# A two-layer trunk on one core: smaller sets of weight tiles, sums on VectorE, 1/rms by tokens, three plain pairs

## The chip, the cores and the metric

The kernel runs on one core of a Trainium2 chip. The metric is the device time of one execution in microseconds (us); lower is better. Engines are named as the profile names them: PE is TensorE (matmuls), PEld its weight loads, DVE VectorE, ACT ScalarE, POOL GpSimd, SP SyncE, which issues most DMAs. Times in rows of the timeline are counted from the start of the profiled span.

## What is computed

A stack of two layers over 1056 tokens (1024 of a prompt and 32 of a running stream), width 1024. Each layer adds a token mixer and then an MLP to the stream h, and the end is one more rmsnorm:

```python
def rmsnorm(x, g):
    y = x * lax.rsqrt(jnp.mean(x * x, axis=-1, keepdims=True) + EPS)
    return y * g

def short_conv_mixer(h, buf, w_in, conv_w, w_out):      # layer 1's mixer
    bg, cg, u = jnp.split(h @ w_in, 3, axis=-1)
    zc = jnp.concatenate([buf, cg * u], axis=1)
    conv = sum(zc[:, j:j + T] * conv_w[j] for j in range(CONV_W))
    return (bg * conv) @ w_out, zc[:, -(CONV_W - 1):]

for i in range(DEPTH):                                   # layer 0: HGRN2 recurrence, layer 1: the convolution
    a = rmsnorm(h, norm_mix[i])
    h = h + mixer_i(a)
    m = rmsnorm(h, norm_mlp[i])
    h = h + jnp.square(jax.nn.relu(m @ w_up[i])) @ w_down[i]    # 1024 -> 4096 -> 1024
return rmsnorm(h, norm_final), new states
```

All is float32 in and out.

## The kernel before

**Number format.** TensorE multiplies in a shortened float32 (`float32r`). Every operand is therefore split into a high part (a cast on ScalarE) and a low part (operand minus high part, on VectorE), and each product is three matmuls: low weights by high activations, high by low, high by high. For weights, `wsplit` does it: a DMA from SP into a tile `raw`, the cast to `whi` (L93), the subtraction into `wlo` (L94). These tiles come from the pool `ws`, which has five `whi`, five `wlo` and four `raw` of 1024 columns; a new one waits until the oldest is no longer read. For activations `split` does it: `xh[k]` on ScalarE (L182), `xl[k]` on VectorE (L183). h is kept transposed in eight tiles `hT[m]`, 128 channels by 1056 tokens.

**The MLP** (L763 to L914) goes through the hidden width in chunks of 256 channels. A group is: two up stages for a chunk (L107 to L109, 72 matmuls each), the two down stages of the chunk before, and the sums of the new one. A down stage is a 2x2 block product done with 7 instead of 8 block multiplications (L803 to L823): seven steps, each for p = 0 and 1, each of six matmuls into a PSUM tile that lives over several steps; after a step its result is added to hT, by VectorE straight from PSUM (L823), or, for steps 0 and 6, by a ScalarE copy out of PSUM (L710) and a GpSimd add (L711). The sums of weight blocks are GpSimd adds (L722) between two splits (L719 and L720, L723 and L724); those of activations are VectorE's (L749), with splits at L745 and L746. PSUM holds four tiles of two banks, all shared. Weights are asked for two stages ahead (`ready` in `mlp`). In layer 0 the last chunk's down product is done plainly: two stages make the eight rows m of hT, drained by VectorE (L840, L841), row m needing the tiles of row m - 2.

**The hand-over.** As soon as a row of hT is final, `fin0(m)` runs for it: `nrm2.add(m)` squares it on ScalarE (L649) and adds the square to a sum on GpSimd (L650), `split_h` makes xh and xl (L182, L183), and a GpSimd DMA parks the row. After every second row `tsums` makes the activation sums that the convolution's products need: scaling on ScalarE (L941), four adds on GpSimd (L943), three splits (L934 with L935, L931 with L932).

**The convolution's products** (L1125 to L1162) are twelve pairs. A plain pair is 192 matmuls (`pair_plain`), one with sums 168 (`pair_sums`); the weights of pair n + 1 are fetched and prepared (`cplain`, `csums`) while pair n multiplies. In pair 0, before its last block row of the first half, `nrm2.scale` makes 1/rms of every token as a full 128 x 1056 tile: three fp32 matmuls with a matrix of ones (L659), VectorE's scaling out of PSUM (L660) and ten more VectorE operations of 1056 columns (L134 to L139). The kernel's start does the same in another way already: `tok_rsqrt` sums over channels with the tokens on the partitions (L153, results of nine columns) and `tok_spread` spreads them again (L171 makes nine diagonal tiles, L172 multiplies them by ones).

**What sets the order.** The program is traced through a tile framework. A list scheduler orders each engine's queue from data dependences, the tracing order and estimated times; every engine then works its queue strictly in that order, with semaphores between engines. So where an instruction stands in its engine's queue is a result of the schedule, and moves when tiles or other instructions change.

## Time and profile before

| | |
|---|---|
| time, median of three runs | 2424.72 us (2424.23 to 2427.03) |
| the profiled execution | 2425.81 us, span 2424.1 us, mean granted TensorE clock 0.991 |
| busy: PE, DVE, ACT, POOL | 2364.3, 1773.4, 835.0, 805.1 us |
| layer 0's mixer, output product and first up stages | 0 to 647.6 us |
| layer 0's MLP from its first down stage | 647.6 to 1292.1 us |
| its plain stage | 1292.1 to 1324.8 us |
| the convolution's twelve pairs | 1324.8 to 1592.3 us |
| layer 1's output product and first up stages | 1592.3 to 1732.7 us |
| layer 1's MLP to its last 7-product down stage | 1732.7 to 2334.1 us |
| its last two chunks and the final norm | 2334.1 to 2424.1 us |

How to read the rows: a row of the view of waits names the engine and what it made, then what it waited for, then us in total, times and the longest. A row of the timeline is the start, the duration, the engine, the source line, the operation, `out<-in`, partitions x elements, and `xN` where N neighbours are merged; in brackets stands the idle time before it and what ended that. A row that counts forms gives the shortest, median and longest duration in ns. Matmul rows overlap, so a pace is read from starts.

### The profile page before, as it was taken

Reading aid. Unit: us, or ns where it says so; the run is one execution under the profiler, and the core shown is the slowest. Engines: PE = TensorE matmul, PEld = TensorE weight load, DVE = VectorE, ACT = ScalarE, POOL = GpSimd, SP = SyncE. Lnnn points to the kernel's source line nnn. Section 1 sums busy time; section 2 is a strip of 40 time slices with the busy share of each in tenths; the row PEclk is TensorE's granted clock in tenths of the full one; section 3 lists DMA queues with packets and bytes.
Section 4 is the critical chain, followed back from the end, with each engine's and each line's share of the span. In section 5 each row is a group of like instructions: output and inputs, shape, how many; then the busy total and the mean of one; then the engine's idle time right before and its main releaser. Section 6 shows DMA issues by size and latency. Waiting matters only on the chain.

```text
span 2424.1 us, 39880 instructions
## 1 busy us (share of the span) xinstructions
PE 2364.3 (98%) x16628; PEld 2339.6 (97%) x16628; DVE 1773.4 (73%) x2522; ACT 835.0 (34%) x1395; POOL 805.1 (33%) x837
## 2 busy tenths in 40 slices
PE   8999999999999999999998899999999999999998
PEld 8999999989999999999998899999999999999997
DVE  8876767644887877877878877644877877878855
ACT  5222222223333333333335433333433333333334
POOL 3110101022243544534537300012344534535523
PEclk9999999999999999999999999999999999999999
DMA  4101011131111111111112122231111111111102
GB/s 170 39 29 49 30 48 30 48 109 44 36 44 53 50 47 49 48 44 53 44 44 98 36 71 89 67 146 44 39 49 47 51 44 53 45 44 53 45 27 72
DMA packets 39221, 135.02 MB, mean 56 GB/s; under 512 B 4720, under 2 KB 7936, under 8 KB 39040
## 3 DMA queue, kind: packets, MB, share of 16 engines
q1 hardware_dynamic: 33632, 113.58, 14.3%
q0 software_dynamic: 5408, 18.89, 2.0%
q8 instruction: 130, 2.13, 0.4%
q14 instruction: 51, 0.42, 0.1%
HBM read 120.57 MB, written 11.88 MB: 55 GB/s over the span
## 4 chain that ended last, share of the span: by engine, by line
PE 89%; DVE 6%; ACT 2%; POOL 1%; issue 0%; DMA 0%; DVEq 0%; SPq 0%; ACTq 0%
PE pb L814 19%; PE pb L107 13%; PE pb L108 13%; PE pb L109 13%; PE pb L1033 10%; PE pj L107 4%; PE pj L108 4%; PE pj L109 4%; DVE wlo L720 2%; DVE hT L823 1%; PE v L498 1%; PE v L497 1%; DVE B L746 1%; PE v L499 1%; ACT whi L719 1%; ACT st L710 1%
## 5 line engine op out<-in xcount | busy, mean ns | idle before, releaser
L107 PE MATMUL pb<-xh,wlo 128*128 128x384 f32 (+1 forms) x1968 | 642.0, 326 | 6.1 <-DVE hT L841 3.7
L109 PE MATMUL pb<-xh,whi 128*128 128x384 f32 (+1 forms) x1968 | 637.6, 324 | 0.0
L108 PE MATMUL pb<-xl,whi 128*128 128x384 f32 (+1 forms) x1968 | 637.5, 324 | 0.0
L711 POOL TENSOR_TENSOR hT<-hT,st 128x528 f32<-128x528 f32 x232 | 375.8, 1642 | 670.4 <-ACT st L710 670.4
L823 DVE TENSOR_TENSOR hT<-hT,pb 128x528 f32<-128x528 f32 x580 | 383.9, 696 | 8.5 <-PE pb L814 0.4
L107 PEld LDWEIGHTS pb<-xh,wlo 128*128 128x128 f32 x1968 | 371.2, 189 | 8.6 <-DVE hT L841 4.0
L109 PEld LDWEIGHTS pb<-xh,whi 128*128 128x128 f32 x1968 | 371.3, 189 | 0.3
L108 PEld LDWEIGHTS pb<-xl,whi 128*128 128x128 f32 x1968 | 371.4, 189 | 0.1
L722 POOL TENSOR_TENSOR raw<-raw 128x256 f32<-128x256 f32 x232 | 227.4, 980 | 68.6 <-DVE wlo L720 57.1
L814 PE MATMUL pb<-B,whi 128*128 128x264 f32 x1392 | 226.0, 284 | 0.0
L93 ACT CAST whi<-raw 128x1024 fp32r<-128x1024 f32 (+1 forms) x119 | 123.7, 1043 | 273.3 <-PE pb L814 143.7
L789 DVE SCALAR_TENSOR_TENSOR u<-pb,nr 128x768 f32<-128x768 f32 x120 | 82.2, 703 | 166.5 <-PE pb L109 166.5
L814 PEld LDWEIGHTS pb<-B,whi 128*128 128x128 f32 x1392 | 192.6, 188 | 0.0
L107 PE MATMUL pj<-xh,wlo 128*128 128x384 f32 (+1 forms) x536 | 177.9, 332 | 7.3 <-ACT xh L182 7.3
L108 PE MATMUL pj<-xl,whi 128*128 128x384 f32 (+1 forms) x536 | 173.4, 324 | 0.0
L109 PE MATMUL pj<-xh,whi 128*128 128x384 f32 (+1 forms) x536 | 173.1, 323 | 0.0
L94 DVE TENSOR_TENSOR wlo<-raw,whi 128x1024 fp32r<-128x1024 f32 (+1 forms) x119 | 146.6, 1237 | 31.2 <-ACT whi L93 30.8
L814 PE MATMUL pb<-B,wlo 128*128 128x264 f32 x696 | 144.2, 288 | 21.3 <-DVE hT L823 21.3
L790 ACT ACTIVATE u<-u 128x768 f32<-128x768 f32 (+1 forms) x128 | 82.3, 643 | 212.8 <-DVE u L789 207.6
L814 PE MATMUL pb<-T,whi 128*128 128x264 f32 x928 | 150.8, 284 | 0.0
L814 PE MATMUL pb<-Q,whi 128*128 128x264 f32 x928 | 150.5, 284 | 0.0
L710 ACT COPY st<-pb 128x528 f32<-128x528 f32 x232 | 133.0, 600 | 46.0 <-PE pb L814 34.3
(284 smaller groups left out, 4637.1 us busy)
## 6 DMA issues: line engine op xcount, KB each, us to landing
raw<-in_wg_up_dram SPq DMA_DIRECT2D x64, 512.0 KB, 3.5
raw<-in_wg_down_dram SPq DMA_DIRECT2D x64, 512.0 KB, 3.5
raw<-in_wg_in_hgrn_dram SPq DMA_DIRECT2D x31, 512.0 KB, 4.3
raw<-in_wg_in_conv_dram SPq DMA_DIRECT2D x24, 512.0 KB, 3.5
xk<-in_x_t_dram SPq DMA_DIRECT2D x8, 528.0 KB, 8.7
hT<-in_x_t_dram POOLq DMA_DIRECT2D x8, 528.0 KB, 6.4
park<-hT POOLq DMA_DIRECT2D x8, 528.0 KB, 3.0
hT<-park POOLq DMA_DIRECT2D x8, 528.0 KB, 7.1
```

What stands on the lines that cost most here:

```text
L93: nc.scalar.copy(hi, raw)
L94: nc.vector.tensor_tensor(lo, raw, hi.bitcast(F32), op=ALU.subtract)
L107: nc.tensor.matmul(ps, wlo, ah, start=start, stop=False)
L108: nc.tensor.matmul(ps, whi, al, start=False, stop=False)
L109: nc.tensor.matmul(ps, whi, ah, start=False, stop=stop)
L710: nc.scalar.copy(q2(st), v)
L711: nc.gpsimd.tensor_tensor(d, d, st, op=op)
L722: nc.gpsimd.tensor_tensor(raw[:, d], raw[:, d], raw[:, o], op=ALU.add)
L790: nc.scalar.activation(u[:, sl], u[:, sl], AF.Square)
L814: nc.tensor.matmul(t[:, q, :QT], wf, xf[:, q * QT : (q + 1) * QT], start=start and n == 0, stop=n == 2, skip_group_check=True)
L823: nc.vector.tensor_tensor(q2(d), q2(d), v, op=op)
L1033: nc.tensor.matmul(t[:, q, :QT], w, v[:, q * QT : (q + 1) * QT], start=start and n == 0, stop=stop and n == 2, skip_group_check=True)
```

## The change

- The pool of weight tiles shrinks: four `whi` and `wlo`, three `raw`. What only the convolution needs has tiles of its own: the sums of its weights (`wsum`), and the hi and lo part of a pair's seventh factor (`whi22`, `wlo22`, two each).
- The four adds of `tsums` go from GpSimd to VectorE. `tsums` is no longer called in `fin0` but behind pairs 0 and 1, and is held back so that it is scheduled behind the instruction noted in `behind[0]`, the low part of the last row's split.
- In pair 0 `nrm2.scale` is replaced by `tok_rsqrt` (in the second half of the pair, at its third block row of the first token half) and `tok_spread` (the same of the second token half), with copies out of PSUM and the square on ScalarE.
- Pair 2 becomes plain as well (`PLAIN` 3 for 2), and `reader` gets the branch for it. `t4` follows pair 2.

```diff
...
     cp = ctx.enter_context(tc.tile_pool(name="cp", bufs=1))
     xs = ctx.enter_context(tc.tile_pool(name="xs", bufs=1))
-    ws = ctx.enter_context(tc.tile_pool(name="ws", bufs=5))
+    ws = ctx.enter_context(tc.tile_pool(name="ws", bufs=4))
     fp = ctx.enter_context(tc.tile_pool(name="fp", bufs=18))
     pj_cm = tc.tile_pool(name="pj", bufs=3, space=PSUM)
     pj = pj_cm.__enter__()
...
     def wtiles():
-        return (ws.tile([P, 4, 256], F32, tag="raw", name="raw", bufs=4),
+        return (ws.tile([P, 4, 256], F32, tag="raw", name="raw", bufs=3),
                 ws.tile([P, 4, 256], F32R, tag="whi", name="whi"),
                 ws.tile([P, 4, 256], F32R, tag="wlo", name="wlo"))
...
         rsqrt(v, y, t)
         return y
-    def tok_spread(y, n):
+    def tok_spread(y, n, new=lambda: ft("dg")):
         out = []
         for g0 in range(0, n, 512):
             ps = newps()
             for b in range(g0 // P, min(-(-n // P), g0 // P + 4)):
                 w = min(P, n - b * P)
-                dg = ft("dg")
+                dg = new()
                 nc.vector.tensor_scalar(dg[:w, :w], ident[:w, :w], y[:w, b : b + 1], None, op0=ALU.mult)
                 nc.tensor.matmul(ps[:, b * P - g0 : b * P - g0 + w], ones[:w, :], dg[:w, :w], start=True, stop=True)
             out.append((g0, min(512, n - g0), ps))
...
     parky = [dp.tile([P, NTOK], F32, name=f"parky{m}") for m in range(4)]
     half = lambda t, h: t[:, h * HALF : (h + 1) * HALF]
     TS = [{} for _ in range(4)]
+    behind = [None]
     def tpart(h, l, src, neg=False):
         if neg:
...
         for j in range(2):
             nc.scalar.activation(u[j], u[j], AF.Copy, scale=vec[:, V_NMIX + 8 + 2 * p + j : V_NMIX + 9 + 2 * p + j])
         (b11, b12), (b21, b22) = [[half(t, h) for h in range(2)] for t in u]
-        add = lambda d, a, b, op: nc.gpsimd.tensor_tensor(d, a, b, op=op)
+        add = lambda d, a, b, op: nc.vector.tensor_tensor(d, a, b, op=op)
         add(b22, b12, b22, ALU.subtract)
         add(b12, b11, b12, ALU.subtract)
         add(b11, b22, b11, ALU.subtract)
...
     def fin0(m):
         nrm2.add(m)
         split_h(m, V_NMIX + 8)
+        behind[0] = nc.cur_bb.bb.instructions[-1]
         nc.gpsimd.dma_start(out=park[m], in_=hT[m])
-        if m % 2:
-            tsums(m // 2)
     mlp(0, nrm, fin0, False)
...
         es = cv.tile([P, KT, 4], F32, name="es")
         nc.gpsimd.tensor_copy(es[:, :, 0:2], vec[:, V_SC : V_SC + 16].rearrange("p (j m) -> p m j", m=KT))
         flat = lambda t: t.rearrange("p a b -> p (a b)")
-        rawt = lambda: ws.tile([P, 4, 256], F32, tag="raw", name="raw", bufs=4)
+        rawt = lambda: ws.tile([P, 4, 256], F32, tag="raw", name="raw", bufs=3)
         hilo = lambda: [flat(ws.tile([P, 4, 256], F32R, tag=t, name=t)) for t in ("whi", "wlo")]
+        hilo22 = lambda: [cv.tile([P, 512], F32R, tag=t + "22", name=t, bufs=2) for t in ("whi", "wlo")]
         q4 = lambda t, i: t[:, i * 512 : (i + 1) * 512]
         def cfetch(n):
...
         def csums(n):
             r0, r1 = cfetch(n)
-            s = flat(rawt())
+            s = cv.tile([P, 1024], F32, name="wsum")
             a11, a12, a22, a21 = q4(r0, 0), q4(r0, 1), q4(r1, 0), q4(r1, 1)
             s1, s4 = q4(s, 0), q4(s, 1)
             add = lambda d, a, b: nc.vector.tensor_tensor(d, a, b, op=ALU.add)
...
             def put(f, src):
                 n = len(w)
                 if n % 2 == 0:
-                    t[:] = hilo()
+                    t[:] = hilo() if n < 6 else hilo22()
                 w[f] = [q4(x, n % 2) for x in t]
                 tpart(*w[f], src)
...
                 ps = [pt() for h in range(2)]
                 order = [(k, h) for k in range(KT) for h in range(2)] if mid and i == 0 else [(k, h) for h in range(2) for k in range(KT)]
                 for n, (k, h) in enumerate(order):
-                    if mid and i == 0 and n == 2 * KT - 2:
-                        mid()
+                    if mid and i == 1 and n % KT == 2:
+                        mid[n // KT]()
                     b = BLK[(i, k % 2)]
                     wt = [q4(x, b % 2)[:, k // 2 * P : (k // 2 + 1) * P] for x in w[b // 2]]
                     mm_h(ps[h], wt, (half(xh[k], h), half(xl[k], h)), k == 0, k == KT - 1)
...
                     if scaled:
                         nc.vector.tensor_tensor(half(d0, h), half(d0, h), t[h], op=ALU.mult)
                 elif to == "d":
-                    nc.scalar.copy(q2(half(d0, 1)), v)
+                    d = q2(half(d0, 1))
+                    if scaled:
+                        nc.vector.tensor_tensor(d, d, v, op=ALU.mult)
+                    else:
+                        nc.scalar.copy(d, v)
                 elif to in ("e", "f"):
                     d = half(d1, "ef".index(to))
                     nc.vector.tensor_tensor(q2(d), q2(d), v, op=ALU.mult)
...
             nc.vector.tensor_scalar(e, es[:, m, 0:2], w(0), None, op0=ALU.mult)
             stt(e, es[:, m, 1:3], 1)
             stt(e, es[:, m, 2:4], 2)
-            nc.vector.tensor_tensor(z[:, :NTOK], ct, nrm2.r, op=ALU.mult)
+            nc.vector.tensor_tensor(z[:, :NTOK], ct, sc["r"], op=ALU.mult)
         sc = {}
+
+        def norm_tok():
+            sc["y"] = tok_rsqrt(mp, (nrm2.acc,), NTOK)
+
+        def norm_spread():
+            r = mp.tile([P, NTOK], F32, tag="nr", name="nr")
+            for g0, n, ps in tok_spread(sc["y"], NTOK, lambda: st()):
+                nc.scalar.copy(r[:, g0 : g0 + n], ps[:, :n])
+            r2 = mp.tile([P, NTOK], F32, tag="acc", name="r2")
+            nc.scalar.activation(r2, r, AF.Square)
+            sc.update(r=r, r2=r2)
+
         pairs = [p for m in range(0, KT, 2) for p in ((m, m), (m + 1, m + 1), (m, m + 1))]
-        PLAIN = 2
+        PLAIN = 3
         ready = {0: cplain(0)}
         ys = {}
         for n, (m, m1) in enumerate(pairs):
...
             else:
                 rd = reader(zt[m][:, :NTOK], zt[m1][:, :NTOK], True)
             if n < PLAIN:
-                pair_plain(w, rd, nrm2.scale if n == 0 else None)
+                pair_plain(w, rd, (norm_tok, norm_spread) if n == 0 else None)
             elif n < len(pairs) - 1:
                 pair_sums(w, rd)
             else:
...
                     nc.gpsimd.dma_start(out=ys[k], in_=parky[k])
                 pair_sums(w, rd, (0, 1, 5, 2, 3, 4, 6))
-            if n == 0:
-                sc["r2"] = mp.tile([P, NTOK], F32, tag="acc", name="r2")
-                nc.scalar.activation(sc["r2"], nrm2.r, AF.Square)
-            if n == PLAIN - 1:
-                for p in range(4):
-                    t4(p)
             if m == m1:
                 conv(m)
             else:
...
                         nc.gpsimd.dma_start(out=parky[k], in_=zt[k][:, :NTOK])
                     else:
                         ys[k] = zt[k][:, :NTOK]
+
+            for p in {0: (0, 1), 1: (2, 3)}.get(n, ()):
+                with tc.issue_after(behind[0]):
+                    tsums(p)
+            if n == PLAIN - 1:
+                for p in range(4):
+                    t4(p)
         nc.gpsimd.dma_start(out=s_conv, in_=zs.rearrange("p j m -> p (j m)"))
         ks = (1, 3, 5, 0, 2, 4, 6, 7)
         for k in ks:
```

The queues show where the schedule puts things. Names in the rows: `hT`, `xl`, `whi` as above, `pb` a PSUM tile, `u` a hidden chunk, `B11` to `T4` the activation factors, `tt` and `ty` the nine-column tiles of 1/rms, `st` a scratch tile; the number behind a name tells the buffer. Line numbers in rows of the change are those of the changed kernel (one or more higher from L925 on; L935 becomes L936, L943 becomes L944).

**VectorE, a group of layer 0's MLP, where the first down stage ends and the second begins.** Before:

```order
L823 TENSOR_TENSOR hT3_5517<-hT3_5517,pb_9095 128x528
L823 TENSOR_TENSOR hT0_5261<-hT0_5261,pb_9163 128x528
L94 TENSOR_TENSOR wlo_9199<-raw_9197,whi_9198 128x1024
L823 TENSOR_TENSOR hT2_5435<-hT2_5435,pb_9171 128x528
L720 TENSOR_TENSOR wlo_9342<-raw_9340,whi_9341 128x768
L823 TENSOR_TENSOR hT5_5693<-hT5_5693,pb_9223 128x528
L746 TENSOR_TENSOR B22_9318<-u_9074,B22_9318 128x528
L823 TENSOR_TENSOR hT7_5869<-hT7_5869,pb_9231 128x528
```

With the change:

```order
L823 TENSOR_TENSOR hT3_5517<-hT3_5517,pb_9095 128x528
L823 TENSOR_TENSOR hT0_5261<-hT0_5261,pb_9163 128x528
L94 TENSOR_TENSOR wlo_9081<-raw_9079,whi_9080 128x1024
L823 TENSOR_TENSOR hT2_5435<-hT2_5435,pb_9171 128x528
L94 TENSOR_TENSOR wlo_9199<-raw_9197,whi_9198 128x1024
L823 TENSOR_TENSOR hT5_5693<-hT5_5693,pb_9223 128x528
L823 TENSOR_TENSOR hT7_5869<-hT7_5869,pb_9231 128x528
L823 TENSOR_TENSOR hT4_5611<-hT4_5611,pb_9203 128x528
```

L720 (first split of the next down stage's weights) and L746 are gone from between the second stage's L823; the L720 comes thirteen rows further down, in the sums. In its place stands an L94, and the L94 that came with the start of the first down stage (`wlo_9081`) has moved down to its end, so both splits of the next up stages' weights are here.

**VectorE, the plain stage of layer 0's MLP, rows 2 to 6.** Before:

```order
L183 SCALAR_TENSOR_TENSOR xl2_83<-hT2_5435,vec_96,xh2_75 128x1056
L840 TENSOR_TENSOR hT4_5611<-hT4_5611,pb_13035 128x768
L183 SCALAR_TENSOR_TENSOR xl3_84<-hT3_5517,vec_96,xh3_76 128x1056
L935 TENSOR_TENSOR Q1_12955<-hT0_5261,Q1_12955 128x528
L841 TENSOR_TENSOR hT4_5611<-hT4_5611,pb_13036 128x288
L935 TENSOR_TENSOR Q2_12958<-hT0_5261,Q2_12958 128x528
L932 SCALAR_TENSOR_TENSOR T3_12961<-hT1_5341,T3_12961 128x528
L840 TENSOR_TENSOR hT5_5693<-hT5_5693,pb_13063 128x768
L841 TENSOR_TENSOR hT5_5693<-hT5_5693,pb_13064 128x288
L840 TENSOR_TENSOR hT6_5787<-hT6_5787,pb_13106 128x768
L183 SCALAR_TENSOR_TENSOR xl4_85<-hT4_5611,vec_96,xh4_77 128x1056
```

With the change:

```order
L183 SCALAR_TENSOR_TENSOR xl2_83<-hT2_5435,vec_96,xh2_75 128x1056
L183 SCALAR_TENSOR_TENSOR xl3_84<-hT3_5517,vec_96,xh3_76 128x1056
L840 TENSOR_TENSOR hT4_5611<-hT4_5611,pb_13005 128x768
L841 TENSOR_TENSOR hT4_5611<-hT4_5611,pb_13006 128x288
L840 TENSOR_TENSOR hT5_5693<-hT5_5693,pb_13033 128x768
L841 TENSOR_TENSOR hT5_5693<-hT5_5693,pb_13034 128x288
L183 SCALAR_TENSOR_TENSOR xl4_85<-hT4_5611,vec_96,xh4_77 128x1056
L840 TENSOR_TENSOR hT6_5787<-hT6_5787,pb_13061 128x768
L183 SCALAR_TENSOR_TENSOR xl5_86<-hT5_5693,vec_96,xh5_78 128x1056
L841 TENSOR_TENSOR hT6_5787<-hT6_5787,pb_13062 128x288
L840 TENSOR_TENSOR hT7_5869<-hT7_5869,pb_13083 128x768
```

The splits Q1, Q2 and T3 of the sums stood between the drains (L840, L841); with the change only the rows' own splits L183 do.

**VectorE, pair 0 of the convolution, ahead of the first diagonal tile.** Before:

```order
L183 SCALAR_TENSOR_TENSOR xl7_88<-hT7_5869,vec_96,xh7_80 128x1056
L935 TENSOR_TENSOR Q1_13097<-hT4_5611,Q1_13097 128x528
L935 TENSOR_TENSOR Q2_13100<-hT4_5611,Q2_13100 128x528
L932 SCALAR_TENSOR_TENSOR T3_13103<-hT5_5693,T3_13103 128x528
L660 TENSOR_SCALAR nv_13295<-pb_13296 128x384
L660 TENSOR_SCALAR nv_13295<-pb_13297 128x288
L935 TENSOR_TENSOR wlo_13204<-raw_13197,whi_13203 128x1024
L935 TENSOR_TENSOR Q1_13168<-hT6_5787,Q1_13168 128x528
L935 TENSOR_TENSOR Q2_13171<-hT6_5787,Q2_13171 128x528
L932 SCALAR_TENSOR_TENSOR T3_13174<-hT7_5869,T3_13174 128x528
```

With the change:

```order
L138 SCALAR_TENSOR_TENSOR tt_13266<-tt_13266,ty_13265 128x9
L944 TENSOR_TENSOR hT5_5693<-hT5_5693,hT4_5611 128x528
L139 SCALAR_TENSOR_TENSOR ty_13265<-tt_13266,ty_13265 128x9
L936 TENSOR_TENSOR Q1_13685<-hT4_5611,Q1_13685 128x528
L137 TENSOR_TENSOR tt_13266<-tv_13264,ty_13265 128x9
L936 TENSOR_TENSOR Q2_13688<-hT4_5611,Q2_13688 128x528
L138 SCALAR_TENSOR_TENSOR tt_13266<-tt_13266,ty_13265 128x9
L933 SCALAR_TENSOR_TENSOR T3_13691<-hT5_5693,T3_13691 128x528
L139 SCALAR_TENSOR_TENSOR ty_13265<-tt_13266,ty_13265 128x9
L944 TENSOR_TENSOR hT6_5787<-hT6_5787 128x528
L171 TENSOR_SCALAR st_13340<-ident_89,ty_13265 128x128
L171 TENSOR_SCALAR st_13343<-ident_89,ty_13265 128x128
```

Before, L660 (1/rms out of PSUM) followed the third set of splits. With the change the nine-column operations of 1/rms alternate with the adds and splits of the sums, L944 and L936, all of which stand behind the last L183; L171 comes after them. In this queue 24 operations of 528 columns lie between the last L183 and the first L171.

## The prediction

> **What bounds the kernel now.** I read the totals first, then TensorE's own waits, then the timeline around each wait.
>
> ```profile
> PE 2364.3 (98%) x16628; PEld 2339.6 (97%) x16628; DVE 1773.4 (73%) x2522; ACT 835.0 (34%) x1395; POOL 805.1 (33%) x837
> ...
> PE pb L814 <- DVE hT L823: 21.3, 28, 1.3
> PE pb L659 <- POOL acc L650: 4.5, 1, 4.5
> PE pb L107 <- DVE hT L841: 3.7, 1, 3.7
> PE pb L1033 <- DVE xl L183: 2.8, 1, 2.8
> PE pb L107 <- DVE hT L840: 2.4, 1, 2.4
> PE pb L659 <- DVE nv L660: 1.1, 1, 1.1
> ```
>
> The first row is busy time, share and instructions; the others say who waits for whom: us in total, times, longest. TensorE sets the time: it is 98% busy, so a gain needs fewer matmuls or less of its waiting. The change touches two kinds of wait. One recurs in the MLP's down stages: 28 times, 21.3 us. The other is one bad stretch where layer 0's MLP hands over to the convolution: 4.5 + 3.7 + 2.8 + 2.4 + 1.1 = 14.5 us.
>
> One MLP group near the start of its second down stage, from the timeline (start us, duration, engine, line; "x9" merges nine rows):
>
> ```profile
> 1235.12 1.33 ACT L710 COPY st<-pb 128x528 f32<-128x528 f32 x2 [1.14 <-PE pb L814]
> 1235.49 0.70 DVE L823 TENSOR_TENSOR hT<-hT,pb 128x528 f32<-128x528 f32 x1
> 1235.64 0.41 PE L814 MATMUL pb<-B,wlo 128*128 128x264 f32 x2
> 1235.79 4.62 POOL L711 TENSOR_TENSOR hT<-hT,st 128x528 f32<-128x528 f32 x3 [5.38 <-ACT st L710]
> 1237.21 2.02 DVE L720 TENSOR_TENSOR wlo<-raw,whi 128x768 fp32r<-128x768 f32 x1 [1.02 <-ACT whi L719]
> 1239.15 0.69 DVE L823 TENSOR_TENSOR hT<-hT,pb 128x528 f32<-128x528 f32 x1
> 1239.76 1.22 DVE L746 TENSOR_TENSOR B<-u,B 128x528 fp32r<-128x528 f32 x1
> 1240.02 0.41 PE L814 MATMUL pb<-B,wlo 128*128 128x264 f32 x2
> 1240.90 5.60 DVE L823 TENSOR_TENSOR hT<-hT,pb 128x528 f32<-128x528 f32 x9
> 1241.65 0.51 PE L814 MATMUL pb<-B,wlo 128*128 128x264 f32 x2 [0.74 <-DVE hT L823]
> ...
> L720 DVE TENSOR_TENSOR wlo<-raw,whi x58: 940/2042/2102, 599.8 to 2293.4; 128x768 fp32r<-128x768 f32 x58
> L943 POOL TENSOR_TENSOR hT<-hT,hT x12: 1311/1436/2353, 1307.5 to 1352.4; 128x528 f32<-128x528 f32 x12
> ```
>
> The down stage starts at 1235.64. From there to 1240.02 lie 36 matmuls in 4.38 us: 0.122 each, 0.73 for a block of six. The next block is due at 1240.75 and starts at 1241.65, 0.90 late, of which 0.74 shows as idle. It needs a PSUM bank that the second L823 empties (1240.90 + 0.70), and VectorE held that one behind L720 (till 1239.23) and L746 (till 1240.98). Both read two SBUF operands, and both are slow here. The last two rows give least/median/most in ns: L720 takes 0.94 when alone and mostly 2.04; a GpSimd add of 528 columns takes 1.31 alone, but the three L711 take 4.62. So each waits for the other's running instruction, while L823, which reads one operand from PSUM, stays at 0.69. The Trainium skill, "SBUF — State Buffer", section "Who interferes with whom", states such an exclusion between VectorE with two SBUF inputs and a GpSimd read, for the whole instruction; the trace agrees (2.04 against 0.94).
>
> **The MLP groups.** In the new order neither L720 nor L746 stands between the down stage's start and its late block. In their place comes the second L94 (weights of the next group): L823, L94, L823, L823. Its whi cast (L93) needs a tile that is free after the first down stage's last matmul, 1235.64, and stands behind the two L710 on ScalarE, 1235.12 to 1236.45. The same pair of operations two microseconds earlier:
>
> ```profile
> 1232.92 1.05 ACT L93 CAST whi<-raw 128x1024 fp32r<-128x1024 f32 x1 [4.93 <-PE pb L814]
> 1234.36 1.22 DVE L94 TENSOR_TENSOR wlo<-raw,whi 128x1024 fp32r<-128x1024 f32 x1
> ```
>
> So the cast ends near 1237.45. GpSimd's adds start at 1235.79 and take 1.3 each: the second is running and ends near 1238.3. L94 waits for that, then takes 1.22: 1239.5. The first L823 ends near 1240.15, the second near 1240.8. TensorE's block due at 1240.02 is 0.13 late, the next not later still. Bounds: 0 (no add in the way) and 0.90 (nothing won). I take 0.13, because L720 in the same place waited for one add only and GpSimd's third let it pass. Each stall shrinks by 0.77. Layer 0 has 14: **-10.8**. Its last down stage (the wait of 1.3) loses a third: **-0.4**. Layer 1 has 13: **-10.0**; 27 x 0.74 + 1.3 is the row of 21.3. Layer 1's last down stage does not stall now:
>
> ```profile
> 2323.92 6.23 POOL L711 TENSOR_TENSOR hT<-hT,st 128x528 f32<-128x528 f32 x4 [5.38 <-ACT st L710]
> 2325.43 2.24 DVE L855 TENSOR_TENSOR gl<-u,gh 128x1056 fp32r<-128x1056 f32 x1 [1.14 <-PE pb L814]
> 2327.59 4.99 DVE L823 TENSOR_TENSOR hT<-hT,pb 128x528 f32<-128x528 f32 x8
> ```
>
> There the second L94 comes between L855 and L823, where nothing is idle. It costs 1.22 alone and up to 2.55 behind a whole add; below, 0 if TensorE had slack. I take 2.4, since four adds run back to back there: **+2.4**.
>
> What moves away must still land in time. L720 now comes in the sums behind both down stages; its user starts after two up stages, each of 72 matmuls or four times the 18 of 2.91 us timed below, 23 us later. The weights of L94 serve the first and second of these up stages, 7 us or more away. VectorE is idle 27% of the time, so this costs 0; the bound is rival (d).
>
> **The hand-over.** The span split by stage (span; then busy PE, PEld, DVE, ACT, POOL; granted clock), and the rows behind its waits:
>
> ```profile
> 1292.10:1324.80 32.70, 26.60 (x146) 25.86 (x145) 26.82 (x26) 19.18 (x21) 26.21 (x17) 0.84 0.26 99
> 1324.80:1592.30 267.50, 259.06 (x2082) 256.33 (x2081) 199.19 (x266) 97.22 (x145) 44.80 (x66) 0.98 0.25 87
> ...
> 1297.92 0.33 PE L107 MATMUL pb<-xh,wlo 128*128 128x384 f32 x1
> 1300.83 0.33 PE L107 MATMUL pb<-xh,wlo 128*128 128x384 f32 x1
> 1319.81 0.69 PE L107 MATMUL pb<-xh,wlo 128*128 128x384 f32 x1 [2.42 <-DVE hT L840]
> 1323.82 0.45 PE L107 MATMUL pb<-xh,wlo 128*128 128x288 f32 x1
> 1343.29 2.61 PE L659 MATMUL pb<-acc,ones 128*128 128x384 f32 x4 [4.47 <-POOL acc L650]
> ...
> 1312.18 2.41 POOL L650 TENSOR_TENSOR acc<-acc,sq 128x1056 f32<-128x1056 f32 x1
> 1332.05 0.94 DVE L840 TENSOR_TENSOR hT<-hT,pb 128x768 f32<-128x768 f32 x1
> 1332.91 2.78 DVE L183 SCALAR_TENSOR_TENSOR xl<-hT,vec,xh 128x1056 fp32r<-128x1056 f32 x1
> 1335.62 0.44 DVE L841 TENSOR_TENSOR hT<-hT,pb 128x288 f32<-128x288 f32 x1
> 1335.98 1.30 DVE L183 SCALAR_TENSOR_TENSOR xl<-hT,vec,xh 128x1056 fp32r<-128x1056 f32 x1
> ```
>
> The plain stage makes eight rows; one takes 1300.83 - 1297.92 = 2.91, eight take 23.3, the stage 32.7. Of the 9.4 over, 6.1 are its two waits (3.7 and 2.4) and the rest is a slow restart: from 1319.81 to 1323.82 twelve matmuls take 4.01, 0.33 each instead of 0.17, and the granted clock is 0.84. GpSimd is busy 26.2 of 32.7: its sixteen L943 adds hold up VectorE's L183 (2.78 for 1.30), and the drains L840 and L841 queue behind these.
>
> Afterwards no L943 and no Q or T split stands among them. VectorE has 0.94 + 0.44 + 1.30 = 2.7 a row against TensorE's 2.9, and GpSimd keeps L650, 2.4 a row, for which about every second L183 waits (+1.4). Row 4's drain stands behind the splits of rows 2 and 3, one held, and these behind ScalarE's square and cast of row 3; row 6 needs row 4's bank one row's time later. I put that 1.8 late. Bounds: 0, and the old 9.4. 23.3 + 1.8 = 25.1, against 32.7: **-7.6**.
>
> **The convolution.** Twelve pairs are 2 x 192 + 10 x 168 = 2064 matmuls now and 3 x 192 + 9 x 168 = 2088 with three plain. At 0.1218 that is 251.4 and 254.3, +2.9. The stage takes 267.4; the other 16.0 are three waits (2.8, 4.5, 1.1), L659's matmuls (2.61 for four of the six records) and slow restarts. The token-wise 1/rms has been run once already, at the kernel's start:
>
> ```profile
> 35.12 1.99 PE L153 MATMUL pj<-ones,acc 128*128 128x1 f32 x18
> 38.43 0.15 DVE L134 TENSOR_SCALAR ty<-tv 128x9 int32<-128x9 int32 x1
> 42.56 1.79 DVE L171 TENSOR_SCALAR dg<-ident,ty 128x128 f32<-128x128 f32 x9
> 42.98 2.36 PE L172 MATMUL pj<-dg,ones 128*128 128x128 f32 x18
> ```
>
> 1.99 + 2.36 = 4.35 of matmuls replace L659's. The new wait is L172 for L171. TensorE gets there 186 matmuls and L153 after the stage's first: 22.7 + 2.0 = 24.7. VectorE has, in that time, the last drains (2.1), a weight split held by an add (3), two L183 (1.3, and 2.8 held): 9.2. Then, ahead of L171, come 24 operations of 528 columns (nine chained L823 take 5.60: 0.62 each, 14.9), two weight splits (2.4, and 2.2 for one add) and a dozen of nine columns at 0.08, the spacing behind 38.43: 20.5 in all. 29.7 - 24.7 = 5.0 of waiting. Bounds: 0, if no add stands in the way of any, and 10, if two more do. A restart like the one at 1319.81 adds 12 x 0.16 = 2. The Trainium skill, "TensorE: Matmul & The Clock Gate", "Part 1: The HAM clock gate (the "warmup" mystery)", has about 3.4 us of idling halve the clock and 3.4 us of work restore it; by that the restart would be an estimated 1.7, and the row shows it after 2.42 idle already. After: 254.3 + 4.3 + 5.0 + 2 = 265.6: **-1.8**. L153 itself needs the last L650, due 13 us into the stage; three adds at 2.4 to 3.4 behind the last drain just fit.
>
> Sum: -10.8 - 0.4 - 10.0 + 2.4 - 7.6 - 1.8 = **-28.2**. The profiled execution took 2425.81 (span 2424.1), 1.1 above the median of 2424.72. From the median: **2396.5**.
>
> **Rivals.** Of a measurement of this kernel about 0.2%, 4.8 us, can be told from no change.
>
> (a) *The group stall stays.* If L94 ends near 1240.2, the first L823 is 0.9 late in place of the second: 2424.7 - 7.6 - 1.8 + 2.4 = 2418. For it: L94 reads two SBUF operands and runs beside the adds, like L720. Against: only one add is under way when its cast is done. 6%.
>
> (b) *The hand-over costs more:* L172 waits 10 and row 6 waits 4: 2396.5 + 5 + 2.2 = 2404. For it: VectorE has 30 us of work ahead of L171 and any held split adds to it. 10%.
>
> (c) *Slower.* L94 loses to two adds: the third is queued when the second ends. Then L94 ends at 1238.3 + 1.31 + 1.22 = 1240.85 and the first L823 at 1241.55; TensorE is 1.6 late in place of 0.90: 27 x 0.7 = +19, and with -7.0 from the rest 2437. It decides once L94 ends after about 1240.5 (27 x 0.26 eats the 7.0). Against: L720 and L746 had to wait for one add each. The page on SBUF of the Trainium skill says only that whoever starts first has the ports, which leaves this open. 6%.
>
> (d) *The smaller set of tiles makes weights late*, and the change does not do what it should: a cast that waits for a tile still in use, 1 us a group, costs 27: 2424. Against: the 7 us of slack or more. 4%.
>
> **Numbers.** The forecast has 74%: 2396.5, its own range 2388 (no wait at L172 nor row 6) to 2406. With (b) 84%. The range 2388 to 2411 leaves out (a), (c), (d) and tails. Faster 0.90 (forecast, a, b), same 0.04 (d), slower 0.06 (c).
>
> **What would show it.** Right: the wait of L814 for L823 falls from 21.3 to under 7 us in all, and one of 2 to 3 is near the end of the second MLP; the plain stage lasts 24 to 27; a wait for L171 of 3 to 7 is new in the first pair; GpSimd has no L943. Wrong: in a group the second L94 ends over 4.6 us after the second down stage's start; or TensorE waits for a weight split.

## The result

The change takes 2400.31 us (median of five, 2399.91 to 2401.85) against 2424.39 before on the same chip: the ratio is 0.990, 95% interval 0.9887 to 0.9916, and the gain 24.1 us. The forecast was 2396.5, a gain of 28.2.

The span of the profiled execution went from 2424.1 to 2398.4. Split as the table of before, view by stages of the change (span; busy PE, PEld, DVE, ACT, POOL; granted clock; DMA share; GB/s):

```profile
0.00:645.40 645.40, 632.96 (x4324) 621.11 (x4325) 438.85 (x895) 180.43 (x422) 110.03 (x277) 0.99 0.17 56
645.40:1278.90 633.50, 632.52 (x4514) 629.64 (x4513) 486.33 (x598) 236.51 (x359) 286.54 (x231) 1.00 0.16 50
1278.90:1305.70 26.80, 23.47 (x147) 23.24 (x146) 22.93 (x21) 20.02 (x21) 17.47 (x12) 1.00 0.43 161
1305.70:1574.30 268.60, 264.45 (x2136) 263.56 (x2135) 192.17 (x284) 95.19 (x142) 26.05 (x54) 0.98 0.24 85
1574.30:1714.70 140.40, 140.40 (x863) 139.08 (x863) 72.01 (x81) 42.74 (x50) 27.81 (x15) 1.00 0.13 41
1714.70:2308.70 594.00, 591.75 (x4225) 589.10 (x4224) 454.60 (x558) 222.55 (x338) 267.44 (x214) 1.00 0.16 50
2308.70:2398.40 89.70, 77.70 (x489) 75.95 (x487) 48.15 (x102) 35.07 (x62) 24.13 (x20) 0.94 0.16 55
```

| stage | before | after | moved | forecast |
|---|---|---|---|---|
| to the first down stages | 647.6 | 645.4 | -2.2 | 0 |
| layer 0's MLP groups | 644.5 | 633.5 | -11.0 | -11.2 |
| plain stage | 32.7 | 26.8 | -5.9 | -7.6 |
| convolution's pairs | 267.5 | 268.6 | +1.1 | -1.8 |
| output product, first up stages | 140.4 | 140.4 | 0 | 0 |
| layer 1's MLP groups | 601.4 | 594.0 | -7.4 | -7.6 |
| rest | 90.0 | 89.7 | -0.3 | 0 |

The first row's 2.2 lies in the first 43 us: TensorE comes to the L153 of the kernel's start at 35.1 us before and at 33.7 with the change, and behind it runs at half pace in the first only (last section). In `nostage_b`, a run below whose program up to there is that of the kernel before, it comes at 33.8 and runs at full pace. So I count the 2.2 to the executions and not to the change; the medians differ by 24.1, the spans by 25.7.

TensorE's waits, us in total, times, longest (the first two rows are the kernel's start and the recurrence, as before):

```profile
PE pj L107 <- ACT xh L182: 6.8, 1, 6.8
PE oT L375 <- DVE ory L368: 4.3, 1, 4.3
PE pb L172 <- DVE st L171: 4.2, 1, 4.2
...
PE pb L107 <- DVE hT L840: 3.3, 1, 3.3
PE pb L814 <- DVE hT L823: 3.2, 2, 2.2
```

The 28 waits of L814 for L823 are two, and no L650 or L183 is left. New is the wait for L171.

One MLP group, the same place as in the prediction:

```profile
1223.00 1.33 ACT L710 COPY st<-pb 128x528 f32<-128x528 f32 x2 [1.14 <-PE pb L814]
1223.37 0.70 DVE L823 TENSOR_TENSOR hT<-hT,pb 128x528 f32<-128x528 f32 x1
1223.53 0.41 PE L814 MATMUL pb<-B,wlo 128*128 128x264 f32 x2
1223.68 6.17 POOL L711 TENSOR_TENSOR hT<-hT,st 128x528 f32<-128x528 f32 x4 [5.33 <-ACT st L710]
1224.22 1.05 ACT L93 CAST whi<-raw 128x1024 fp32r<-128x1024 f32 x1
1225.31 2.07 DVE L94 TENSOR_TENSOR wlo<-raw,whi 128x1024 fp32r<-128x1024 f32 x1 [1.24 <-ACT whi L93]
1227.30 5.61 DVE L823 TENSOR_TENSOR hT<-hT,pb 128x528 f32<-128x528 f32 x9
1228.04 0.51 PE L814 MATMUL pb<-B,wlo 128*128 128x264 f32 x2
```

The down stage starts at 1223.53. L94 ends at 1227.38, 3.85 later (forecast 3.86), and TensorE's block starts 4.51 after the stage, 0.13 behind its pace of 4.38. So L94 did wait for one add (2.07 for 1.22), and no more.

### The profile page after: what moved, and what is told of

Its sections match the earlier page's. It is cut to its first block, busy times and chain, and to the rows that moved or that the text cites. A ratio compares the mean times of both kernels' runs of the same rounds, so it can differ in the third digit from the quotient of the medians.

```text
span 2398.4 us, 40070 instructions
## 1 busy us (share of the span) xinstructions
PE 2363.2 (99%) x16682; PEld 2341.7 (98%) x16682; DVE 1715.1 (72%) x2534; ACT 832.5 (35%) x1390; POOL 759.5 (32%) x822
## 4 chain that ended last, share of the span: by engine, by line
PE 96%; DVE 3%; issue 0%; ACT 0%; DMA 0%; DVEq 0%; SPq 0%; ACTq 0%
PE pb L814 25%; PE pb L107 14%; PE pb L108 13%; PE pb L109 13%; PE pb L1034 10%; PE pj L107 4%; PE pj L108 4%; PE pj L109 4%; PE v L497 1%; PE v L498 1%; PE v L499 1%; PE aps L389 1%; PE lps L390 1%; PE ups L407 1%; PE ops L432 1%; DVE xl L183 1%
## 5 line engine op out<-in xcount | busy, mean ns | idle before, releaser
L823 DVE TENSOR_TENSOR hT<-hT,pb 128x528 f32<-128x528 f32 x580 | 383.1, 698 | 8.5
L722 POOL TENSOR_TENSOR raw<-raw 128x256 f32<-128x256 f32 x232 | 209.7, 904 | 336.6 <-DVE wlo L720 322.9
L814 PE MATMUL pb<-B,whi 128*128 128x264 f32 x1392 | 225.9, 284 | 0.0
L94 DVE TENSOR_TENSOR wlo<-raw,whi 128x1024 fp32r<-128x1024 f32 (+1 forms) x119 | 171.0, 1441 | 48.5 <-ACT whi L93 48.0
L814 PEld LDWEIGHTS pb<-B,whi 128*128 128x128 f32 x1392 | 192.4, 188 | 0.0
L814 PE MATMUL pb<-T,whi 128*128 128x264 f32 x928 | 150.7, 284 | 0.0
L814 PE MATMUL pb<-Q,whi 128*128 128x264 f32 x928 | 150.6, 284 | 0.0
L814 PE MATMUL pb<-B,wlo 128*128 128x264 f32 x696 | 144.2, 288 | 3.2 <-DVE hT L823 3.2
```

Of the source, the lines that this page charges most:

```text
L94: nc.vector.tensor_tensor(lo, raw, hi.bitcast(F32), op=ALU.subtract)
L722: nc.gpsimd.tensor_tensor(raw[:, d], raw[:, d], raw[:, o], op=ALU.add)
L814: nc.tensor.matmul(t[:, q, :QT], wf, xf[:, q * QT : (q + 1) * QT], start=start and n == 0, stop=n == 2, skip_group_check=True)
L823: nc.vector.tensor_tensor(q2(d), q2(d), v, op=op)
```

## The experiments

All numbers of stages below are read as above, from the first matmul of a stage to the first of the next, out of each kernel's own profiled execution. Times are medians beside the kernel before on the same chip (2422.9 to 2424.6).

| kernel | time | MLP 0 | plain | conv. | MLP 1 |
|---|---|---|---|---|---|
| before | 2424.4 | 647.5 | 32.7 | 267.4 | 601.4 |
| the change | 2400.3 | 636.5 | 26.8 | 268.6 | 594.0 |
| w_only | 2407.7 | 636.6 | 32.1 | 268.6 | 595.2 |
| h_only | 2420.1 | 647.6 | 28.4 | 266.9 | 601.6 |
| ws4_raw4 | 2404.7 | 636.6 | 36.1 | 263.3 | 595.4 |
| plain2 | 2395.8 | 636.6 | 26.8 | 264.3 | 593.8 |
| pooladds | 2413.9 | 636.6 | 29.3 | 278.8 | 593.9 |
| oldnorm | 2399.0 | 636.6 | 28.3 | 266.2 | 593.9 |
| spread_late | 2399.3 | 636.6 | 28.3 | 266.2 | 594.0 |
| act_behind | 2396.6 | 636.6 | 28.3 | 263.0 | 593.9 |
| gl_behind | 2397.7 | 636.6 | 26.8 | 268.5 | 591.6 |
| best_a | 2391.4 | 636.6 | 28.2 | 259.2 | 591.4 |
| nostage_b | 2398.5 | 634.1 | 35.2 | 266.7 | 588.0 |
| best_n5 | 2389.1 | 634.1 | 30.0 | 262.5 | 588.2 |

MLP 0 is counted here from the very first matmul of its first down stage (644.6 us before, 642.4 with the change), and in the tables above from some 3 us later. `oldnorm`, `spread_late`, `act_behind` and `gl_behind` ran twice, `nostage_b` once, the others four times or more; each has one profile.

The clock alone moves a stage by about 1.5 us from one profile to another. Behind the same wait of 3.3 us in the plain stage the granted clock stays at 1.00 in the change, `plain2` and `gl_behind`, and the stage takes 26.8; in `h_only`, `oldnorm` and `spread_late` it falls to about 0.5 for some 3 us, and the stage takes 28.3 or 28.4. The convolution has such a place too (last section). A difference of that size in one of these two stages says nothing of an edit by itself.

**The two halves alone.** `w_only` puts the weight tiles of the change into the kernel before; `h_only` is the change with the old tiles.

```diff
# w_only, on the kernel before
-    ws = ctx.enter_context(tc.tile_pool(name="ws", bufs=5))
+    ws = ctx.enter_context(tc.tile_pool(name="ws", bufs=4))
...                                  # raw: bufs=4 -> 3; wsum, whi22, wlo22 as in the change
# h_only, on the change
-    ws = ctx.enter_context(tc.tile_pool(name="ws", bufs=4))
+    ws = ctx.enter_context(tc.tile_pool(name="ws", bufs=5))
...                                  # raw: bufs=3 -> 4; wsum, whi22, wlo22 taken from the pool again
```

> The kernel before with part 1 alone: four whi and wlo, three raw, the convolution's own wsum and whi22/wlo22. Theory (the MLP gain comes from the weight tiles alone, since fewer tiles change where VectorE's queue has its weight splits): layer 0's MLP -11, layer 1's MLP -7.4, the hand-over as before (14.5 us of waits, plain stage 32.7): 2424.4 - 18.4 = 2406. Rival (the parts need each other: with the sums still in the hand-over, the smaller set starves the convolution's weights): the same MLP gain, but the convolution 3 us or more longer: 2409 or above. Rival (no gain without the other parts): 2424.

> The change without part 1: sums on VectorE behind the last row, 1/rms by tokens, three plain pairs, but five whi/wlo and four raw as before. Theory: the MLP groups keep their 0.74 us waits; the plain stage gains 5.9 and the convolution loses 1.1, as in the change: 2424.4 - 4.8 = 2419.6. Rival (the gain in the groups belongs to the load on GpSimd or to the whole change): 2406 or less.

`w_only`: 2407.68, ratio 0.9933 (0.9918 to 0.9948). `h_only`: 2420.07, ratio 0.9984 (0.9975 to 0.9993). TensorE's waits, first two rows of `w_only`, then one of `h_only`:

```profile
PE pb L814 <- DVE hT L823: 3.2, 2, 2.3
PE pb L659 <- POOL acc L650: 4.5, 1, 4.5
```

```profile
PE pb L814 <- DVE hT L823: 21.3, 28, 1.3
```

The groups' gain (10.9 and 6.2) is the tiles' alone, and the hand-over's gain (4.4) is the rest's. Layer 1 gains 7.4 in the change and 6.2 here, but a group takes 43.9 in both; the 1.2 lies in the last down stage, which takes 24.5 in `w_only` and 23.0 in the change, with the same wait of 2.3 or 2.2 and, in `w_only`, a slow clock behind it (0.58 for 3 us, against 1.00). The two gains, 16.8 and 4.4, make 21.2 of the 24.1; the interval of `w_only` alone is 3.6 us to each side, so the rest is not shown to be more than noise.

**Which tiles.**

```diff
# ws4_raw4, on the kernel before: raw stays at bufs=4, wsum stays in the pool
-    ws = ctx.enter_context(tc.tile_pool(name="ws", bufs=5))
+    ws = ctx.enter_context(tc.tile_pool(name="ws", bufs=4))
...                                  # whi22, wlo22 as in the change
```

> The kernel before with four whi and wlo but four raw as before (and whi22/wlo22 apart). Theory: the number of whi/wlo tiles decides, because the cast into whi is what waits for TensorE to have read a tile: 2406, as with three raw. Rival: three raw tiles hold the DMA back and this moves the splits: 2424, the 0.74 us waits all there.

2404.74, ratio 0.9922 (0.9905 to 0.9939): MLP 636.6 and 595.4 with four raw tiles too. So three raw tiles are not what decides; the number of whi and wlo is. (Both runs also have whi22 and wlo22 apart, which only the convolution uses; five tiles with these apart were not tried.) VectorE's queue shows it in the schedule: with four, the second L94 takes the place of L720 and L746 in the second down stage, with four raw or three.

**The third plain pair.**

```diff
# plain2, on the change
-        PLAIN = 3
+        PLAIN = 2
```

> The change with pair 2 not plain (168 instead of 192 matmuls). Theory: 24 matmuls less are 2.9 us, but pair 2 then needs the last sums and its own weight sums from a VectorE that is busy without a gap in pairs 0 and 1, so a wait of 2 to 5 us takes the gain back: 2399 to 2402. Rival (the sums are done in time, the third plain pair is a pure loss): 2397.4. Rival (the wait is far longer): 2405 or more.

2395.82, ratio 0.9887 (0.9873 to 0.9902), 4.5 us under the change. The rival holds: pair 2 waits for nothing, and TensorE's waits are those of the change. The stage is 264.3 instead of 268.6. 24 matmuls at 0.122 are 2.9 of these 4.3; the rest goes with a shorter slow stretch behind the wait (the eighteen L172 take 3.7 for 4.1, and the product's matmuls behind them are back at full pace sooner), which is the clock and not shown to be the edit's. So this part of the change was a plain loss.

**Adds back on GpSimd.**

```diff
# pooladds, on the change, in tsums
-        add = lambda d, a, b, op: nc.vector.tensor_tensor(d, a, b, op=op)
+        add = lambda d, a, b, op: nc.gpsimd.tensor_tensor(d, a, b, op=op)
```

> The change with the sixteen adds of the sums back on GpSimd (still traced behind pairs 0 and 1). One of the first four now stands among the squares' adds of the plain stage, the other fifteen after it. Theory (adds on GpSimd hold up VectorE's splits and the other way round, so that each of the 16 costs VectorE up to 1.3 us): the plain stage 27 to 30 us, L171 2 to 8 us later, time 2403 to 2409. Rival (it is the place of the adds behind the last row that matters, not the engine; VectorE has 16 operations of 0.62 less): 2396 to 2400.

2413.89, ratio 0.9961 (0.9941 to 0.998): 13.6 over the change, beyond the theory's 2403 to 2409. TensorE's waits, and two rows of VectorE:

```profile
PE pb L172 <- DVE st L171: 6.5, 3, 5.2
PE pb L1034 <- ACT z L1082: 5.0, 1, 5.0
...
1318.95 4.73 DVE L936 TENSOR_TENSOR Q<-hT,Q 128x528 fp32r<-128x528 f32 x2
1341.58 3.03 DVE L171 TENSOR_SCALAR st<-ident,ty 128x128 f32<-128x128 f32 x4
```

Two splits take 4.73 where they take 1.31 without adds beside them, four L171 3.03 for 0.85. Of the hand-over's parts tried one by one, the engine of the adds is worth the most. Its two stages take 29.3 + 278.8 = 308.1 here, against 295.4 in the change and 300.1 in the kernel before: with the adds left on GpSimd the rest of the new hand-over is a loss.

**1/rms as before.**

```diff
# oldnorm, on the change
-                pair_plain(w, rd, (norm_tok, norm_spread) if n == 0 else None)
+                pair_plain(w, rd, norm_full if n == 0 else None)    # nrm2.scale() and the square, in pair 0's first half
```

> The change with 1/rms made as before (Norm.scale, in the first half of pair 0) and not by tokens. Saved: L153 1.9, L172 4.1, its wait 4.3 and the slow clock behind L153, 1.6. Paid: L659's matmuls 3.1, a wait for the last L650 (done 12.9 us into the stage, wanted 11), and the third L659 behind VectorE's L660, which now stands behind seven adds and splits of the sums, 6 to 7 us. Theory (the token-wise form is worth little by itself, it trades one wait for another): 2398 to 2402. Rival (the ten full-width operations of 1.25 us delay the sums so that pair 3 waits): 2405 or more. Rival (L660 comes in time): 2393.

2399.04 (2398.76 and 2399.32): the token-wise form gains nothing here. The row `L659 <- nv L660` takes over:

```profile
PE pb L659 <- DVE nv L660: 4.9, 1, 4.9
```

**Three waits of the change, one by one.**

```diff
# spread_late: tok_spread in the middle of pair 1's first half, conv(0) behind pair 1
+                pair_plain(w, rd, {0: {(1, 2): norm_tok}, 1: {(0, 8): norm_spread}}.get(n), n == 0)
# act_behind: L942 too queued behind the last row's cast (behind[0] is then ScalarE's, behind[1] VectorE's)
+        behind[:] = nc.cur_bb.bb.instructions[-2:]
+                with tc.issue_after(behind[0]), tc.issue_after(behind[1]):
# gl_behind: gsplit queued behind the last VectorE instruction of the down stage
+                with tc.issue_after([i for i in nc.cur_bb.bb.instructions if i.engine == mybir.EngineType.DVE][-1]):
```

> The change with tok_spread moved from the second half of pair 0 to the middle of pair 1's first half (and conv(0) behind pair 1). VectorE reaches the first L171 30.2 us into the convolution's stage in the run of the change; TensorE would now come to L172 33 us into it. Theory (the wait L172 for L171, 4.2 us, is on the path; with it go a slow restart of 1 and the slow clock under L172 itself, 1.5): the convolution's stage 268.6 - 6.7 = 262, time 2394. Rival (VectorE is the bound there, the wait moves to the next drain or to conv(0) and conv(1) ahead of pair 2): 2399 to 2401.

2399.28 (2398.18 and 2400.39). The wait stayed:

```profile
1337.59 1.05 PE L172 MATMUL pb<-st,ones 128*128 128x128 f32 x8
1342.60 2.64 PE L172 MATMUL pb<-st,ones 128*128 128x128 f32 x10 [3.95 <-DVE st L171]
```

The first four tiles (two records each) now come in time, but there are four scratch tiles, and VectorE makes the next five 7.4 us after the first four, behind sums that the schedule put between. The rival was right that VectorE is the bound, the place it named was not.

> The change with ScalarE's eight scalings of the sums (L942) also queued behind the last row's cast. In the change two of them stand between the casts of rows 1 and 2, the second waiting 1.43 us for a split. Theory (these push rows 2 and 3's splits and so row 4's drain; TensorE's 3.3 us wait in the plain stage comes from them in part): the wait falls to 1 to 2 us, the plain stage from 26.8 to about 25. The scalings then delay the sums, so that L171 comes up to 2 us later. Time 2398 to 2400. Rival (the wait comes from the held L183 alone, 4.24 us for two): the wait stays at 3.3.

2396.55 (2396.07 and 2397.02). The plain stage's wait fell from 3.3 to 2.3, but 2.4 more appeared ahead of the convolution's first product, where pair 0 needs a bank that L840 empties. So the stage takes 28.3 at a clock of 1.00, 1.5 more than in the change and not the expected 25: there the theory missed. The gain lies in the convolution, against the expectation: the wait for L171 is gone. The scalings being later, the schedule sets fewer sums ahead of L171 (27.0 us into the stage for 30.2), and L172 runs at 1.32 for five tiles.

> The change with the gate splits (L855) of the second MLP's last chunk but one queued behind the last L823 of its last 7-product down stage. Theory (L855 and L94 stand one after the other ahead of L823, each held by a GpSimd add; this costs TensorE 2.2 us): the wait falls to 0.1, layer 1's MLP stage from 594.0 to 591.7, time 2398. Rival (the splits are then late for the stage that uses them): TensorE waits as long later, 2400.

2397.71 (2397.69 and 2397.73). As the theory has it: MLP 1 591.6 for 594.0, and

```profile
PE pb L814 <- DVE hT L823: 1.0, 1, 1.0
```

**The three edits that paid, together** (`plain2`, `act_behind`, `gl_behind`).

> Three edits on the change: two plain pairs, ScalarE's scalings behind the last row's cast, the gate splits behind the last 7-product down stage. If the gains of the single runs add (4.5, 3.8 and 2.6): 2400.3 - 10.9 = 2389.4. If the scalings' gain was the L172 wait, which two plain pairs do not touch, and the last sums now come too late for pair 2, a wait of some us appears at pair 2: 2391 to 2395.

2391.39, ratio 0.9868 (0.9852 to 0.9885): 8.9 of the 10.9 added gains, or 7.5 when each kernel is taken against the one before on its own chip (31.6 and 24.1 under it). No wait of pair 2 appears.

**No adds on GpSimd in the MLP.** On the kernel before:

```diff
-    STAGED = (0, 6)
+    STAGED = ()
```

> The kernel before without the ScalarE copies and GpSimd adds of steps 0 and 6: all fourteen results of a down stage are added by VectorE. No GpSimd add runs in the down stages then. Theory (the 2.04 us of L720 and the 1.22 of L746 are waits for GpSimd's adds): L720 0.94, L746 0.70 in all groups. VectorE has 14 x 0.62 + 1.2 = 9.9 us of a down stage's 10.2, so it may become the bound; time 2400 to 2430. Rival (their length comes from something else, as the tile's size or PSUM traffic): L720 stays at 2.0 us.

2398.52 (one execution), just under the 2400 to 2430 expected. Durations in ns (least, median, most), and a wait:

```profile
L720 DVE TENSOR_TENSOR wlo<-raw,whi x58: 943/952/959, 598.0 to 2275.1; 128x768 fp32r<-128x768 f32 x58
L94 DVE TENSOR_TENSOR wlo<-raw,whi x119: 425/1219/1266, 3.9 to 2320.2; 128x1024 fp32r<-128x1024 f32 x117, 128x256 fp32r<-128x256 f32 x1, 128x768 fp32r<-128x768 f32 x1
L823 DVE TENSOR_TENSOR hT<-hT,pb x812: 695/698/707, 643.7 to 2307.5; 128x528 f32<-128x528 f32 x163
...
PE pb L814 <- DVE hT L823: 1.5, 2, 0.8
```

L720 never takes more than 0.96. It has another place here, and in the change, where it has moved too, it takes mostly 0.96 as well; the stronger sign is L94. It still stands among the L823 of the second down stage, and with no GpSimd add beside it never takes more than 1.27, where it took 2.07 in the change. So what held these operations was GpSimd's adds. VectorE does not become the bound: it does 232 adds more and TensorE waits 1.5 us in all. This one line, without the smaller sets, makes the groups shorter than the whole change does: 634.1 and 588.0. Because the schedule also moved L720 and L746 out of the down stages, the gain is both effects together; what the missing adds are worth with the two at the old place was not tried.

**With the hand-over of the run of three edits,** five whi and wlo tiles, four raw and no staged adds:

> The hand-over of the change with the three edits of the run before (two plain pairs, scalings and gate splits held back), with five whi/wlo and four raw tiles as before the change, and with all results of the down stages added by VectorE. If the group stall is GpSimd's adds alone, the smaller tile sets are not needed: layer 0's MLP 634.1 and layer 1's 588.0 as in the run without these adds on the old kernel, the hand-over as in the run with three edits (28.2 and 259.2): 2391.4 - 2.5 - 3.4 = 2385.5. If five tiles bring the waits back, even so: 2391 to 2400.

2389.10 (2388.64 to 2390.5), ratio 0.9856 (0.9839 to 0.9872), the fastest of all, though its interval overlaps that of the three edits alone. The MLP came out as expected (634.1, 588.2), so the smaller sets are not needed once GpSimd's adds are gone. The hand-over did not (30.0 and 262.5 for 28.2 and 259.2), so the time is above the 2385.5 that was added up: with the old tiles the schedule is another, and TensorE waits 3.3 for L171 again and 4.0 for a drain in the plain stage (2.2 with the three edits).

## Why the prediction was right

The signs it named came: TensorE's wait for L823 is 3.2 us in all (under 7), 2.2 of it near the end of the second MLP; the plain stage lasts 26.8 (24 to 27); the wait for L171 is 4.2 (3 to 7); and no add of the sums runs on GpSimd.

**The groups.** Right in mechanism and size: -11.0 and -7.4 against -11.2 and -7.6. The step that carried it, that L94 waits for the second add and "then takes 1.22", was out by a hundredth of a us. `w_only` and `ws4_raw4` show that the tiles did it, `nostage_b` that the adds are what L94 was waiting for. Rivals (a) and (c) did not come: L94 took 2.07, not 2.8 or more. Nor did (d): no wait of TensorE for a weight split is among those of the change.

**The last down stage of layer 1.** Forecast +2.4:

```profile
2297.72 2.23 DVE L855 TENSOR_TENSOR gl<-u,gh 128x1056 fp32r<-128x1056 f32 x1 [1.11 <-PE pb L814]
2299.87 2.33 DVE L94 TENSOR_TENSOR wlo<-raw,whi 128x1024 fp32r<-128x1024 f32 x1
2302.13 4.38 DVE L823 TENSOR_TENSOR hT<-hT,pb 128x528 f32<-128x528 f32 x7
```

TensorE's wait is 2.2, and `gl_behind` got 2.4 back.

**The plain stage.** Forecast -7.6, measured -5.9. The step that failed is "I put that 1.8 late", a value between two bounds that no sum led to: row 6 waited 3.3. That is nearer to rival (b), which had it wait 4.

```profile
1288.76 1.18 ACT L942 ACTIVATE hT<-hT,vec 128x1056 f32<-128x1056 f32 x1 [0.18 <-DVE hT L840]
1291.37 1.18 ACT L942 ACTIVATE hT<-hT,vec 128x1056 f32<-128x1056 f32 x1 [1.43 <-DVE xl L183]
1292.46 1.07 ACT L649 ACTIVATE sq<-hT 128x1056 f32<-128x1056 f32 x1
1293.43 2.23 ACT L182 ACTIVATE xh<-hT,vec 128x1056 fp32r<-128x1056 f32 x2
...
1294.63 4.24 DVE L183 SCALAR_TENSOR_TENSOR xl<-hT,vec,xh 128x1056 fp32r<-128x1056 f32 x2 [1.70 <-ACT xh L182]
1298.79 0.94 DVE L840 TENSOR_TENSOR hT<-hT,pb 128x768 f32<-128x768 f32 x1
```

I followed the sums' adds and splits out of the stage on VectorE and GpSimd, but not their scalings on ScalarE: `issue_after` holds back one engine, and two L942 stayed ahead of the casts of rows 2 and 3, one of them waiting 1.43 itself. Moving them back (`act_behind`) took 1 us off this wait, so that much of it is shown to be theirs; it did not shorten the stage, since 2.4 us came up behind it. The two splits took 4.24, for the 4.0 that two of 1.30 with 1.4 for "one held" make. What the rest of the 3.3 comes from was not tried. The 26.8 is also lucky: in three other kernels the same wait was followed by a slow clock and the stage took 28.3 or 28.4, and the forecast had no term for that.

**The convolution.** Forecast -1.8, measured +1.1; term by term (us):

| | forecast | measured |
|---|---|---|
| 2088 matmuls | 254.3 | 254.3 |
| L153 | 2.0 | 1.9 |
| wait for L171 (measured from start to start) | 5.0 | 4.3 |
| L172 | 2.35 | 4.1 |
| slow pace besides (measured: the remainder) | 2 | 2.3 |
| output product's matmuls inside the stage | 0 | 1.7 |
| sum | 265.6 | 268.6 |

Two terms failed. The old stage's "other 16.0" held ten matmuls of the next product, 1.7 us, which stay and which I let go with the waits. And L172 was priced at its duration at the kernel's start (2.36), while it runs here right after a wait, at half the clock (0.50 over the 4.7 us from 1336.30). In the timeline of the change on TensorE:

```profile
1336.27 2.47 PE L172 MATMUL pb<-st,ones 128*128 128x128 f32 x10 [4.15 <-DVE st L171]
1339.20 2.04 PE L172 MATMUL pb<-st,ones 128*128 128x128 f32 x8
```

The wait itself came as worked out: VectorE reached L171 30.2 us in, 29.7 forecast, and rival (b)'s 10 did not come. The "+2.9" of the third plain pair was right as a price; I gave no term for what it buys, and `plain2` shows that it buys nothing.

One row was read wrongly: that the slow restart at 1319.81 comes "after 2.42 idle already". In the kernel before the pace had fallen earlier, behind the wait of 3.68:

```profile
1315.58 0.61 PE L107 MATMUL pb<-xh,wlo 128*128 128x288 f32 x1 [3.68 <-DVE hT L841]
1316.46 0.45 PE L107 MATMUL pb<-xh,wlo 128*128 128x288 f32 x1
```

From 1316.22 on these matmuls start 0.24 apart, where the same form stood 0.13 apart before that wait, so the 2.42 found the clock slow already. How long an idle must be to slow it is not shown: behind the same 3.3 us it stayed at 1.00 in three kernels and fell in three others.

The misses add up: 1.7 in the plain stage, 2.9 in the convolution, 0.4 in the two rows of groups, less 0.3 at the end, 4.7 in all; the 2.2 that the start took off go against them, and 2.5 remain, from the forecast's -28.2 to the -25.7 of the two spans. The medians differ by 24.1, mostly since the profiled execution of before took 1.4 more than the median of 2424.39. So the total is closer than its terms: the start's 2.2, which the forecast did not have, hides nearly half of the misses in the spans. The measured 2400.3 lies midway between the forecast and rival (b)'s 2404.

## What to carry to other kernels

A tile set that is one smaller can be faster, because it changes when the scheduler may issue the preparing work; look at what then stands between the instructions that free TensorE's banks. Where VectorE's two-operand work and GpSimd's adds share a stretch, price each at its own time plus the other's running instruction, and try first whether VectorE can do the adds by itself. When several edits come together, run each alone: of the four here the weight tiles gave 17 us, giving the adds back to GpSimd cost 13.6, 1/rms by tokens gave nothing, and the third plain pair cost 4.5.

## What the runs showed that I had not expected

**A slow clock without a wait.** Behind L153 (eighteen records of 128x1 in 1.99 us, busy without a gap), the granted clock fell in the change (first two rows: span, busy, then the clock behind the bracketed counts; third row: the stretch of L172 after its wait). The fourth row is the place behind L153 in `h_only`:

```profile
1319.00:1321.00 2.00, 2.00 (x21) 1.99 (x19) 2.00 (x4) 0.63 (x1) 0.00 (x0) 1.00 0.28 25
1321.00:1325.50 4.50, 4.50 (x26) 4.49 (x27) 4.50 (x8) 3.50 (x6) 0.00 (x0) 0.62 0.27 109
1336.30:1341.00 4.70, 4.70 (x21) 4.48 (x21) 3.44 (x11) 1.74 (x4) 0.00 (x0) 0.50 0.00 0
```

```profile
1334.60:1339.10 4.50, 4.50 (x38) 4.49 (x39) 4.50 (x8) 4.50 (x8) 0.00 (x0) 1.00 0.01 4
```

In the change 4.5 us at a clock of 0.62 hold 26 records, in `h_only` 38 at 1.00: about 1.5 us. `plain2`, `gl_behind` and `act_behind` pay it at this place as the change does, `pooladds`, `spread_late`, `best_a` and `best_n5` do not. That the execution alone can decide it shows at the kernel's start, where the same eighteen records stand in every kernel: the 4.5 us behind them have a clock of 0.62 in the profiles of `before` and `w_only` and of 1.00 in the other twelve, and `nostage_b` has the program of `before` there. The Trainium skill, "TensorE: Matmul & The Clock Gate", "Part 1: The HAM clock gate (the "warmup" mystery)", says that the clock is granted by activity in a window that runs freely; that some executions pay and others don't goes with it, but no run here shows the window.

**A held VectorE instruction can lose several times.** In the groups L94 and L720 never waited for more than one add (at most 2.36 for 1.22, and 2.10 for 0.94). In `nostage_b`, at the hand-over:

```profile
1323.23 5.55 DVE L932 SCALAR_TENSOR_TENSOR T<-hT,T 128x528 fp32r<-128x528 f32 x1
1323.28 1.31 POOL L943 TENSOR_TENSOR hT<-hT,hT 128x528 f32<-128x528 f32 x1
...
1324.56 2.40 POOL L650 TENSOR_TENSOR acc<-acc,sq 128x1056 f32<-128x1056 f32 x1
1326.93 1.29 POOL L943 TENSOR_TENSOR hT<-hT 128x528 f32<-128x528 f32 x1
```

L932, 0.70 alone, was held across three GpSimd adds. So the mechanism of rival (c) exists, only not in the groups. What decides between the two cases is open; it was not tried.
